# Two transformer-like blocks on one core: second projections in pieces between the seven products of a block of the first projection

## The chip, the core and the metric

One core of a Trainium2 chip runs the whole program in one launch. The metric is the device time in microseconds (us) of that launch; lower is better. A core has TensorE (matmuls into PSUM), VectorE, ScalarE and GpSimd, and SyncE, which issues transfers; each engine executes its own queue in order, and the engines meet at semaphores.

## The reference, cut to what matters

Two models follow each other on 512 tokens of width 1024, each with two layers. A layer is a mixer (projections, recurrences, attention) and a feed-forward network. The networks are what the change is about:

```python
# first model, twice, D_FF = 3072
h = rms_norm(x, norm_ffn[l])
ff_g, ff_u = jnp.split(h @ ffn_up[l], 2, axis=-1)
ff_g = causal_dwconv(ff_g, ffn_conv_w[l], ffn_conv_b[l])     # 3 taps along the tokens
x = x + (jax.nn.gelu(ff_g) * ff_u) @ ffn_down[l]
# second model, twice, D_FF_2 = 2816
gu = h @ w_gate_up
x = x + (jax.nn.silu(gu[..., :D_FF_2]) * gu[..., D_FF_2:]) @ w_down
```

All is float32.

## The kernel before, in words

Every large product is made of three float32r matmuls: an operand v is split into a high half (ScalarE rounds it, line 361, tiles named wh, ffh, ...) and a low half (VectorE subtracts, line 369, wl, ffl, ...), and `three` (line 436) adds low x high, high x low and high x high into one PSUM bank.

**Order of work.** The program is written out by a planner at build time. `Issue` (line 98) keeps one clock for each engine and a price for every instruction; of the instructions whose inputs are ready it appends, time after time, the one that could start first, and among those within 0.03 us of that the one of the lowest priority number. So prices and priorities fix the order of every engine's queue. A matmul's price stands in `mmr` (line 431), the priorities in `PRIO` (line 70).

**Units.** The weights come as a list of units, which `drive` (line 556) takes in order with four chains: a loader (SyncE loads a chunk of weights into one of 8 raw buffers, at most 8 units ahead), a splitter (line 593; wh and wl, three buffers each, freed when the unit's matmuls are done), the matmuls (`main`, line 603) and an evacuator (line 625), which hands on a unit's results when slots are free. A split has priority 1 when at least two of the three buffers are free (`split`), and 4 otherwise (`split2`). What follows a product goes into a chain called `behind`, of priority 0.

**A network** (`ffn`, line 1884). The first projection yields column blocks of 256 gate and 256 up columns, 12 blocks in the first model's networks, 11 in the second's. Blocks 0 and 1 are plain. The others (`Block`, line 1792) use a scheme of seven products, P1 to P7, of half size: 24 matmuls of 256 columns each into a bank ps_u. The weights of four of them are made in place: when the buffer has been split, GpSimd issues a transfer that adds another block of the matrix to it (`dma_add`), and the next product that uses the buffer splits it again. P1, P5, P6 and P4 use one buffer in this order, with an add after each of the first three; P7's buffer gets one add before its split.

A block's P1, P2, P5 and P6 alternate with P7, P4 and P3 of the block before, in the loop from line 1942:

```python
            yield B.u["P1"]
            if prev:
                yield prev.u["P7"]
            for d in todo:
                yield from down_units(*d, fs, False)
            todo = []
            yield B.u["P2"]
```

then P5, P4 and P3 of the block before, and P6. After P4, `after_P4` (line 1862) adds into the gate (fg) and calls the gate's `rest`: in the first model ScalarE's first tap, two VectorE taps (fy) and a gelu, in the second a silu. After P3, `after_P3` (line 1870) subtracts into u, multiplies u by the gate and splits the result into ffh and ffl, 128 rows of the second projection's input: two such tiles for a block.

**The second projection** (`down_units`, line 1914) runs on groups of tiles, (6, 6, 6, 6) in the first model and (6, 6, 6, 4) in the second. For a group it makes units of `proj_t` (line 644), each with two banks ps_t of 128x512; for 6 tiles a bank takes two units of 18 matmuls, for 4 tiles one unit of 24. VectorE adds a finished bank to x (x<-x,ps_t). All units of a group follow each other, behind P7.

Of the kernel before, what the change touches and what calls it, by code (L numbers as in the profile page):

```python
# [319 lines left out]
class Unit:  # L320


    def __init__(self, chunk, view, mm, evac=None, ready=None, pre=None, need=4):
        self.chunk, self.view, self.mm, self.evac, self.ready, self.pre = chunk, view, mm, evac, ready, pre
        self.need, self.w, self.then = need, None, None
        chunk.users += 1
# [3 lines left out]
def kernel(ctx, tc, a, out):  # L330
# [100 lines left out]
    def mmr(o, lhsT, rhs, first, last, **kw):  # L431
        order.op("pe", size(rhs) * 0.000445 + 0.004,
                 lambda: nc.tensor.matmul(o, lhsT=lhsT, rhs=rhs, start=first, stop=last, **kw), [o], [lhsT, rhs],  # L433
                 rows=lhsT.shape[0])
# [113 lines left out]
    behind = Chain(None, 0)  # L548

    def after(fn):  # L550

        old, order.cur = order.cur, behind
        fn()
        order.cur = old

    def drive(units):
# [36 lines left out]
        def splitter():  # L593
            for u in each():
                if u is None:
                    yield "wait"
                else:
                    yield from until(lambda: u.chunk.buf is not None and whs.left and wls.left)
                    order.cur.prio = PRIO["split2" if len(whs.left) < NHL - 1 else "split"]
                    split(u)  # L600
                    yield

        def main():
            q = 0
            while st["main"] < len(look) or not st["done"]:
                fill()
                u = look[st["main"]]
                q += 1
                if q in starts:
                    yield from starts[q]  # L610
                if u.pre is not None:
                    yield from u.pre()
                yield from until(lambda: u.w is not None)
                yield from u.mm(u.w[2], u.w[3])
                u.w[0].free()
                u.w[1].free()
                if u.evac is not None:
                    evacs.append(u)
                look[st["main"]] = None
                st["main"] += 1  # L620
                fill()
                yield
            st["over"] = True

        def evacuator():
            while True:
                while not evacs:
                    if "over" in st:
                        return
                    yield "wait"  # L630
                u = evacs.popleft()
                yield from until(lambda: (u.ready is None or u.ready()) and len(slots.left) >= u.need)
                after(u.evac)
                yield
# [9 lines left out]
    def proj_t(w, c0, ntile, src, evac, ready=None, pre=None, ktiles=8, need=3):  # L644

        for i0 in range(0, ntile, 2):
            n = min(2, ntile - i0)
            pss = {}
            if ktiles <= 4:
# [10 lines left out]
                def ev4(i0=i0, n=n, pss=pss):  # L660
                    for i in range(n):
                        evac(i0 + i, pss[i].t)
                        pss[i].free()

                yield Unit(ch, lambda ch=ch: ch.view(), mm4, ev4, ready, pre, need * n)
# [3 lines left out]
            for k0 in range(0, ktiles, kc):  # L669
# [12 lines left out]
                def ev8(i0=i0, n=n, pss=pss):  # L682
                    for i in range(n):
                        evac(i0 + i, pss[i].t)
                        pss[i].free()

                yield Unit(ch, lambda ch=ch: ch.view(), mm8, ev8 if k0 + kt == ktiles else None, ready, pre, need * n)
                pre = None

    def proj_n(w, c0, ncols, src, evac, ready=None, pre=None, ktiles=8, nb=NT):  # L690
# [3 lines left out]
        for k0 in range(0, ktiles, hs):  # L694
# [19 lines left out]
            yield Unit(ch, lambda ch=ch: ch.view(), mm_, ev if k0 + kt == ktiles else None, ready, pre, 0)  # L714
# [366 lines left out]
    def first_mix(l, norm, nxt):  # L1081
# [126 lines left out]
        def unit_small():  # L1208
# [14 lines left out]
            yield Unit(ch, lambda: ch.view(), mm_, lambda: spawn(small_chain(bank[0], r), PRIO["sm"]), rdy if r else None,  # L1223
# [568 lines left out]
    class Block:  # L1792
# [3 lines left out]
        def __init__(self, X, w, cols, gate, done):  # L1796
# [7 lines left out]
            for nm, ch, x, add in (("P1", A, "A11", b12), ("P5", A, "S1", b22), ("P6", A, "S2", b21), ("P4", A, "A22", None),  # L1804
                                   ("P7", T3, "S3", None), ("P2", C21, "A12", None), ("P3", C22, "S4", None)):
                u = self.u[nm] = Unit(ch, ch.view, lambda h, lo, nm=nm, x=x: self.mm(nm, x, h, lo))
                if add is not None:
                    u.then = lambda ch=ch, add=add: dma_add(ch.view(), add)
# [53 lines left out]
        def after_P4(self):  # L1862
# [3 lines left out]
            self.s1.free()  # L1866
            for j in range(2):
                self.g[j] = self.gate.rest(j, self.g[j])

        def after_P3(self):  # L1870
# [3 lines left out]
            self.u2.free()  # L1874
            for j in range(2):
# [8 lines left out]
    def ffn(norm, up, down, ff, groups, gate, fin, late=None):  # L1884
# [55 lines left out]
        prev, todo = None, []  # L1940
        spawn(X.build(norm), 3)
        for b in range(nblk):
            if b < NOLD:
                yield from plain(b, fs)
                continue
# [10 lines left out]
            for d in todo:  # L1956
                yield from down_units(*d, fs, False)
            todo = []
            yield B.u["P2"]
            yield B.u["P5"]  # L1960
# [3 lines left out]
            yield B.u["P6"]  # L1964
            prev = B
            if b - 1 in ends:
                todo.append(ends[b - 1])
        for nm in ("P7", "P4", "P3"):
            yield prev.u[nm]
        for d in todo:  # L1970
            yield from down_units(*d, fs, False)
# [688 lines left out]
    def body():  # L2660
        norm = norm0
        for l in range(2):
# [3 lines left out]
            yield from ffn(nf, a["ffn_up"][l], a["ffn_down"][l], FF1, (6, 6, 6, 6), lambda k0, l=l: Gate1(l, k0), norm.add,  # L2666
                           mem_prep if l == 1 else None)
        for l in range(2):
# [3 lines left out]
            yield from ffn(nf, a["w_gate_up_2"][l], a["w_down_2"][l], FF2, (6, 6, 6, 4), lambda k0: Gate2(),  # L2672
# [32 lines left out]
```

## Time and profile before

| | |
|---|---|
| median of 3 runs | 3403.86 us (3395.11 to 3408.48) |
| the profiled execution, its own time | 3401.47 us |
| its span, first to last instruction | 3399.7 us |
| mean granted TensorE clock | 0.983 |
| busy: TensorE (PE) | 3263.6 us, 96% |
| busy: VectorE (DVE) | 2175.3 us, 64% |
| busy: ScalarE (ACT) | 1574.1 us, 46% |
| busy: GpSimd (POOL) | 358.7 us, 11% |
| moved by DMA | 380.52 MB |

PE is the matmuls and PEld the weight loads of TensorE. A stretch with a granted clock of 1.00 ran at 2.4 GHz throughout, one of 0.50 at 1.2 GHz. Matmuls overlap in the profile, so the duration of one comes from the length of a run of them divided by their number, not from the mean of one. The networks lie at about 640 to 1000, 1640 to 2000, 2400 to 2730 and 3050 to 3400 us; the mixers lie between.

### The profile page before, as it was taken

To read this page: it belongs to the slowest core of one execution; us is meant where nothing else is said; L and a number is where in the kernel's file an instruction comes from. 1 tells how busy PE (TensorE), PEld (TensorE's weight loads), DVE (VectorE), ACT (ScalarE), POOL (GpSimd) and SP (SyncE) were. 2 spreads that over 40 slices of the span, in tenths; PEclk is the share of its full clock that TensorE was granted. 3 is DMA by queue.
4 is the path that set the end of the run, shared out by engine and by line. 5 is a ranking of instruction groups with operands and counts; after the bars stand their busy time and mean duration, and the time that the engine had idled before them with its cause. 6 is when DMAs were issued, how large, how long until landed. Compare 5 with 4: busy or idle time off the path is not lost. (4 is left out here: it accounts for less than half of the span.)

```text
span 3399.7 us, 45909 instructions
## 1 busy us (share of the span) xinstructions
PE 3263.6 (96%) x17637; PEld 2747.4 (81%) x17637; DVE 2175.3 (64%) x4134; ACT 1574.1 (46%) x2711; POOL 358.7 (11%) x407
## 2 busy tenths in 40 slices
PE   9999999999999999999899999999999999999999
PEld 6778778888887778778788888767888878888887
DVE  7973544765677973535765587776655577874554
ACT  6452433443344552433443366766433357743342
POOL 2000000111100000000111112110111111101110
PEclk9999999999999999999999999999999999999999
DMA  4323133466752323132476653211567642236773
GB/s 147 99 69 93 50 106 98 101 154 146 158 131 75 108 63 95 48 112 93 104 158 155 148 135 121 93 51 55 131 148 160 172 142 69 63 86 144 153 158 87
DMA packets 350667, 380.52 MB, mean 112 GB/s; under 512 B 17839, under 2 KB 324768, under 8 KB 350448
## 3 DMA queue, kind: packets, MB, share of 16 engines
q1 hardware_dynamic: 262576, 276.47, 26.3%
q0 software_dynamic: 87840, 101.12, 17.3%
q8 instruction: 138, 2.26, 0.3%
q14 instruction: 81, 0.66, 0.1%
q10 hardware_dynamic: 32, 0.01, 0.0%
HBM read 367.05 MB, written 10.49 MB: 111 GB/s over the span
## 5 line engine op out<-in xcount | busy, mean ns | idle before, releaser
L369 DVE TENSOR_TENSOR wl<-raw,wh 128x1024 fp32r<-128x1024 f32 (+2 forms) x667 | 775.5, 1167 | 675.5 <-ACT wh L361 673.9
L361 ACT ACTIVATE wh<-raw 128x1024 fp32r<-128x1024 f32 (+2 forms) x667 | 672.7, 1014 | 953.3 <-PE ps_t L433 496.9
L433 PE MATMUL ps_u<-xsh,wl 128*128 128x256 f32 x1216 | 363.0, 299 | 91.3 <-DVE wl L369 84.7
L433 PE MATMUL ps_u<-xsh,wh 128*128 128x256 f32 x1216 | 357.4, 294 | 0.0
L433 PE MATMUL ps_u<-xsl,wh 128*128 128x256 f32 x1216 | 357.2, 294 | 0.0
L433 PEld LDWEIGHTS ps_u<-xsh,wl 128*128 128x128 f32 x1216 | 245.0, 201 | 100.9 <-DVE wl L369 91.0
L433 PE MATMUL ps_t<-ffl,wh 128*128 128x512 f32 x736 | 290.4, 395 | 1.5 <-DVE ffl L369 1.5
L433 PE MATMUL ps_t<-ffh,wl 128*128 128x512 f32 x736 | 289.9, 395 | 0.6 <-ACT ffh L361 0.5
L433 PE MATMUL ps_t<-ffh,wh 128*128 128x512 f32 x736 | 290.3, 395 | 0.0
L433 PE MATMUL ps_t<-h2l,wh 128*128 128x512 f32 x704 | 283.8, 403 | 0.0
L433 PE MATMUL ps_t<-h2h,wl 128*128 128x512 f32 x704 | 283.7, 403 | 0.0
L433 PE MATMUL ps_t<-h2h,wh 128*128 128x512 f32 x704 | 281.3, 400 | 0.0
L433 PEld LDWEIGHTS ps_u<-xsl,wh 128*128 128x128 f32 x1216 | 245.8, 202 | 0.0
L433 PEld LDWEIGHTS ps_u<-xsh,wh 128*128 128x128 f32 x1216 | 245.8, 202 | 0.0
L369 DVE TENSOR_TENSOR x<-x,ps_t 128x512 f32<-128x512 f32 x192 | 131.0, 685 | 107.1 <-PE ps_t L433 106.9
L433 PE MATMUL ps_u<-xbh,wl 128*128 128x256 f32 x608 | 172.1, 283 | 6.8 <-DVE wl L369 3.8
L433 PE MATMUL ps_u<-xbl,wh 128*128 128x256 f32 x608 | 171.3, 282 | 0.0
L433 PE MATMUL ps_u<-xbh,wh 128*128 128x256 f32 x608 | 170.8, 281 | 0.0
L416 POOL DMA_DIRECT2D raw<-in_ffn_up_dram x80 | 102.3, 1363 | 630.0 <-DVE wl L369 486.5
L433 PEld LDWEIGHTS ps_t<-ffl,wh 128*128 128x128 f32 x736 | 138.2, 188 | 34.7 <-DVE ffl L369 3.0
L433 PEld LDWEIGHTS ps_t<-ffh,wl 128*128 128x128 f32 x736 | 138.1, 188 | 33.0 <-ACT ffh L361 1.1
L433 PEld LDWEIGHTS ps_t<-ffh,wh 128*128 128x128 f32 x736 | 138.2, 188 | 31.6
(453 smaller groups left out, 7271.0 us busy)
## 6 DMA issues: line engine op xcount, KB each, us to landing
raw<-in_w_in_dram SPq DMA_DIRECT2D x128, 512.0 KB, 3.8
raw<-in_ffn_up_dram SPq DMA_DIRECT2D x96, 512.0 KB, 3.5
raw<-in_w_gate_up_dram SPq DMA_DIRECT2D x88, 512.0 KB, 3.6
raw<-in_ffn_up_dram POOLq DMA_DIRECT2D x80, 512.0 KB, 6.0
raw<-in_w_gate_up_dram POOLq DMA_DIRECT2D x72, 512.0 KB, 6.5
raw<-in_ffn_down_dram SPq DMA_DIRECT2D x64, 384.0 KB, 5.1
raw<-in_w_out_dram SPq DMA_DIRECT2D x40, 512.0 KB, 3.4
raw<-in_w_down_dram SPq DMA_DIRECT2D x48, 384.0 KB, 5.3
```

Of the source, the lines that this page charges most:

```text
L361: lambda: nc.scalar.activation(out=out, in_=in_, func=func, **kw),
L369: dve(0.00104, lambda: nc.vector.tensor_tensor(out=out, in0=in0, in1=in1, op=op), [out], [in0, in1])
L416: order.op("pool", 1.0, lambda: nc.gpsimd.dma_start(out=out, in_=in_, accum_op=ALU.add), [out], [out], extra=max(n, 0.05), slack=0.5)
L433: lambda: nc.tensor.matmul(o, lhsT=lhsT, rhs=rhs, start=first, stop=last, **kw), [o], [lhsT, rhs],
```

## The change

- The loop over the blocks yields one unit of the second projection after P2 and one after P6, as long as the list `todo` has any (`between`). A group goes on that list right after P6 of the block that follows its last block; groups of the plain blocks at once.
- The groups are of four tiles: six in the first model, (4, 4, 4, 4, 6) in the second.
- The split of a product's weights always has priority 1 (`soon`).
- `rest` of the gate (convolution, gelu or silu) and the multiplies and splits after P3 move from `behind` into a chain `later` of priority 2.
- A unit's evacuation is a list with one entry for a tile; each waits for its own slots.
- The planner's price of a matmul of n columns is max(256, n)/2400 + 0.0025 us instead of 0.000445 n + 0.004: 0.2158 instead of 0.2318 for 512 columns, 0.1092 instead of 0.1179 for 256.

```diff
-        order.op("pe", size(rhs) * 0.000445 + 0.004,
+        order.op("pe", max(256, size(rhs)) / 2400.0 + 0.0025,
...
-    behind = Chain(None, 0)
-
-    def after(fn):
-
-        old, order.cur = order.cur, behind
+    behind, later = Chain(None, 0), Chain(None, 2)
+
+    def after(fn, chain=behind):
+
+        old, order.cur = order.cur, chain
...
-                    order.cur.prio = PRIO["split2" if len(whs.left) < NHL - 1 else "split"]
+                    order.cur.prio = PRIO["split2" if len(whs.left) < NHL - 1 and not u.soon else "split"]
...
-                if u.evac is not None:
-                    evacs.append(u)
+                for f in u.evac or ():
+                    evacs.append((u, f))
...
                 u = self.u[nm] = Unit(ch, ch.view, lambda h, lo, nm=nm, x=x: self.mm(nm, x, h, lo))
+                u.soon = True
...
             self.b3.free()
             self.s1.free()
+            after(self.gates, later)
+
+        def gates(self):
             for j in range(2):
                 self.g[j] = self.gate.rest(j, self.g[j])
...
             self.b4.free()
             self.u2.free()
+            after(self.ends, later)
+
+        def ends(self):
...
+        def between():
+
+            while todo:
+                u = next(todo[0], None)
+                if u is not None:
+                    return [u]
+                todo.popleft()
+            return []
+
...
-            for d in todo:
-                yield from down_units(*d, fs, False)
-            todo = []
             yield B.u["P2"]
+            yield from between()
             yield B.u["P5"]
...
             yield B.u["P6"]
+            if b - 1 in ends and b - 1 >= NOLD:
+                todo.append(down_units(*ends[b - 1], fs, False))
+            yield from between()
             prev = B
-            if b - 1 in ends:
-                todo.append(ends[b - 1])
...
-            yield from ffn(nf, a["ffn_up"][l], a["ffn_down"][l], FF1, (6, 6, 6, 6), lambda k0, l=l: Gate1(l, k0), norm.add,
+            yield from ffn(nf, a["ffn_up"][l], a["ffn_down"][l], FF1, (4,) * 6, lambda k0, l=l: Gate1(l, k0), norm.add,
...
-            yield from ffn(nf, a["w_gate_up_2"][l], a["w_down_2"][l], FF2, (6, 6, 6, 4), lambda k0: Gate2(),
+            yield from ffn(nf, a["w_gate_up_2"][l], a["w_down_2"][l], FF2, (4, 4, 4, 4, 6), lambda k0: Gate2(),
```

SyncE's queue in the first network: the loads of first (ffn_up) and second (ffn_down) projection. Before:

```order
L410 DMA raw<-in_ffn_up_dram 128x4x256 x16
L410 DMA raw<-in_ffn_down_dram 128x3x256 x8
L410 DMA raw<-in_ffn_up_dram 128x4x256 x12
L410 DMA raw<-in_ffn_down_dram 128x3x256 x8
L410 DMA raw<-in_ffn_up_dram 128x4x256 x8
```

Now, its beginning:

```order
L410 DMA raw<-in_ffn_up_dram 128x4x256 x10
L410 DMA raw<-in_ffn_down_dram 128x4x256 x2
L410 DMA raw<-in_ffn_up_dram 128x4x256 x3
L410 DMA raw<-in_ffn_down_dram 128x4x256
L410 DMA raw<-in_ffn_up_dram 128x4x256
L410 DMA raw<-in_ffn_down_dram 128x4x256
L410 DMA raw<-in_ffn_up_dram 128x4x256 x4
```

Eight down loads in a row have become single ones between one to four up loads.

VectorE's queue in the last network, around the split for P6 of block 6. Before, where that split is wl_28476, the bank of P4 ps_u_28477, and the bank of P5 and P3 ps_u_28199:

```order
L369 TENSOR_TENSOR fg_28161<-ps_u_28477,s1_28099 128x256
L369 TENSOR_TENSOR fg_28162<-ps_u_28477,s1_28099 128x256
L369 TENSOR_TENSOR u_28374<-ps_u_28199,u2_28293 128x256
L369 TENSOR_TENSOR u_28375<-ps_u_28199,u2_28293 128x256
L369 TENSOR_TENSOR u_28374<-u_28374,fg_28161 128x512
L369 TENSOR_TENSOR u_28375<-u_28375,fg_28162 128x512
L369 TENSOR_TENSOR wl_28476<-raw_28062,wh_28475 128x1024
L369 TENSOR_TENSOR ffl_28505<-u_28374,ffh_28504 128x512
```

Now, where P6's split is wl_28498, the next down unit's wl_28536, the next P1's wl_28564, and the banks are ps_u_28499 (P4) and ps_u_28158 (P5 and P3):

```order
L369 TENSOR_TENSOR wl_28498<-raw_28055,wh_28497 128x1024
L369 TENSOR_TENSOR fg_28086<-ps_u_28499,s1_28021 128x256
L369 TENSOR_TENSOR fg_28087<-ps_u_28499,s1_28021 128x256
L369 TENSOR_TENSOR wl_28536<-raw_28331,wh_28535 128x1024
L369 TENSOR_TENSOR u_28362<-ps_u_28158,u2_28257 128x256
L369 TENSOR_TENSOR u_28363<-ps_u_28158,u2_28257 128x256
L369 TENSOR_TENSOR u_28362<-u_28362,fg_28086 128x512
L369 TENSOR_TENSOR wl_28564<-raw_28364,wh_28563 128x1024
L369 TENSOR_TENSOR ffl_28527<-u_28362,ffh_28526 128x512
```

The split for P6 has moved from behind the subtractions after P3 and the multiplies to ahead of the additions after P4; a multiply and its ffl now stand between later splits.

The first down unit of a fresh group, in the first network after P6 of block 6 (bank ps_t_6697 and ps_t_6698, weights wh_6634 and wl_6635; tiles ff_6309 and ff_6311 are old, ff_6623 and ff_6625 come from the block whose P3 stands just before P6). VectorE's queue now, from the end of that P3 on (fy are the taps, wl_6662 the split for P1, wl_6704 for P7):

```order
L369 TENSOR_TENSOR u_6457<-ps_u_6245,u2_6347 128x256
L373 SCALAR_TENSOR_TENSOR fy_6595<-fg_6173,colt2_97,fy_6595 128x510
L369 TENSOR_TENSOR u_6458<-ps_u_6245,u2_6347 128x256
L369 TENSOR_TENSOR wl_6662<-raw_6459,wh_6661 128x1024
L369 TENSOR_TENSOR u2_6664<-ps_u_6663,s1_6422 128x512
L373 SCALAR_TENSOR_TENSOR fy_6596<-fg_6174,colt3_98,fy_6596 128x511
L369 TENSOR_TENSOR wl_6704<-raw_6492,wh_6703 128x1024
L373 SCALAR_TENSOR_TENSOR fy_6596<-fg_6174,colt2_97,fy_6596 128x510
L369 TENSOR_TENSOR u_6457<-u_6457,fy_6595 128x512
L369 TENSOR_TENSOR u_6458<-u_6458,fy_6596 128x512
L369 TENSOR_TENSOR ffl_6624<-u_6457,ffh_6623 128x512
L369 TENSOR_TENSOR ffl_6626<-u_6458,ffh_6625 128x512
```

Before, three products (P6, P1, P7) stood between the end of such a P3 and the first matmul of a group. TensorE's queue in that unit now, from the last of twelve matmuls on old tiles:

```order
L433 MATMUL ps_t_6698<-ffh_6311,wh_6634 128x512
L433 MATMUL ps_t_6697<-ffh_6623,wl_6635 128x512
L433 MATMUL ps_t_6698<-ffh_6623,wl_6635 128x512
L433 MATMUL ps_t_6697<-ffl_6624,wh_6634 128x512
L433 MATMUL ps_t_6697<-ffh_6623,wh_6634 128x512
L433 MATMUL ps_t_6697<-ffh_6625,wl_6635 128x512
```

The twelve matmuls on old tiles of both banks stand first, and the matmuls on the fresh tiles follow. There are four such units in each of the first model's networks and three in each of the second's, where eighteen matmuls stand ahead of those on the last tile (in the first of the three, eighteen in another order).

## Rows read from the trace of the kernel before

**Rows 1.** Busy time by stage: mixer and network in turn; columns below.

```profile
core 0: us, PE busy (x) PEld busy (x) DVE busy (x) ACT busy (x) POOL busy (x), PEclk, DMA share, GB/s
0.00:640.00 640.00, 625.10 (x2845) 491.94 (x2846) 407.96 (x881) 285.68 (x486) 40.78 (x85) 0.99 0.31 95
640.00:1000.00 360.00, 332.06 (x2186) 306.28 (x2184) 220.73 (x301) 148.64 (x196) 49.79 (x39) 0.96 0.65 145
1000.00:1640.00 640.00, 635.39 (x2863) 496.48 (x2862) 397.55 (x811) 273.43 (x455) 24.05 (x49) 0.99 0.29 86
1640.00:2000.00 360.00, 331.72 (x2203) 305.38 (x2202) 225.83 (x311) 151.55 (x199) 56.01 (x49) 0.97 0.67 148
2000.00:2400.00 400.00, 391.19 (x1908) 313.49 (x1907) 315.98 (x846) 271.21 (x640) 57.13 (x67) 1.00 0.26 81
2400.00:2730.00 330.00, 308.20 (x2024) 282.42 (x2023) 183.81 (x252) 121.67 (x168) 51.63 (x46) 0.97 0.68 155
2730.00:3050.00 320.00, 317.30 (x1524) 257.64 (x1523) 243.11 (x502) 200.73 (x407) 35.10 (x38) 1.00 0.28 89
3050.00:3400.00 350.00, 322.65 (x2097) 293.80 (x2095) 180.37 (x236) 121.24 (x163) 44.18 (x35) 0.97 0.61 135
```

**Rows 2.** Waits of TensorE, whole span: us in total, times, longest.

```profile
PE ps_u L433 <- DVE wl L369: 88.5, 33, 4.8
```

**Rows 3.** Chain of waits, 2540 to 2670: start, length, what.

```profile
2554.48 33.44 PE ps_t L433 x144
2587.92 31.27 PE ps_u L433 x264
...
2619.22 0.48 DVE u L369 x2
...
2620.49 0.68 DVE u L369
2621.17 1.15 DVE wl L369
...
2622.36 16.10 PE ps_u L433 x120
```

**Rows 4.** Busy time over a stretch with two waits; columns as in rows 1.

```profile
2619.00:2659.00 40.00, 33.57 (x243) 32.93 (x242) 23.34 (x31) 15.40 (x21) 7.67 (x6) 0.87 0.70 139
```

**Rows 5.** Timeline of VectorE and GpSimd, a split and the add after it.

```profile
2606.59 1.23 DVE L369 TENSOR_TENSOR wl<-raw,wh 128x1024 fp32r<-128x1024 f32 x1 [1.25 <-ACT wh L361]
...
2608.11 1.26 POOL L416 DMA_DIRECT2D raw<-in_w_gate_up_dram  x1 [6.45 <-DVE wl L369]
```

**Rows 6.** DMA issues, 2588 to 2659, products only: KB, median us to landing.

```profile
raw<-in_w_gate_up_dram POOLq DMA_DIRECT2D x10, 512.0 KB, 6.3
...
raw<-in_w_gate_up_dram SPq DMA_DIRECT2D x5, 512.0 KB, 5.6
```

**Rows 7.** DMA issues, 2554 to 2659, a down projection and products.

```profile
raw<-in_w_gate_up_dram SPq DMA_DIRECT2D x12, 512.0 KB, 3.6
```

**Rows 8.** Groups by form, 755 to 870: busy us, mean ns of one, idle before.

```profile
L369 DVE TENSOR_TENSOR wl<-raw,wh 128x1024 fp32r<-128x1024 f32 x23 | 27.9, 1220 | 11.5 <-ACT wh L361 11.5
L361 ACT ACTIVATE wh<-raw 128x1024 fp32r<-128x1024 f32 x24 | 25.3, 1054 | 17.6 <-PE ps_t L433 9.6 <-PE ps_u L433 3.4 <-issue 3.4
...
L373 DVE SCALAR_TENSOR_TENSOR fy<-fg,colt,fy 128x511 f32<-128x511 f32 x8 | 5.8, 750 | 1.7 <-ACT fy L361 1.7
...
L369 DVE TENSOR_TENSOR x<-x,ps_t 128x512 f32<-128x512 f32 x8 | 5.5, 686 | 6.2 <-PE ps_t L433 6.2
...
L369 DVE TENSOR_TENSOR u<-u,fy 128x512 f32<-128x512 f32 x6 | 3.9, 682 | 0.0
L361 ACT ACTIVATE ffh<-u 128x512 fp32r<-128x512 f32 x6 | 3.7, 628 | 2.1 <-DVE u L369 2.1
L369 DVE TENSOR_TENSOR u<-ps_u,u 128x256 f32<-128x256 f32 x8 | 3.2, 417 | 0.0
```

**Rows 9.** Instructions that write wl, whole span: ns min/median/max, forms.

```profile
L369 DVE TENSOR_TENSOR wl<-raw,wh x667: 557/1218/1258, 9.4 to 3375.6; 128x1024 fp32r<-128x1024 f32 x134, 128x768 fp32r<-128x768 f32 x29, 128x640 fp32r<-128x640 f32 x2, 128x384 fp32r<-128x384 f32 x2
```

More of the change, by code (lines that the diff above doesn't have):

```diff
@@ L324, in __init__ @@
         self.chunk, self.view, self.mm, self.evac, self.ready, self.pre = chunk, view, mm, evac, ready, pre
-        self.need, self.w, self.then = need, None, None
+        self.need, self.w, self.then, self.soon = need, None, None, False
         chunk.users += 1
@@ L630, in evacuator @@
                     yield "wait"
-                u = evacs.popleft()
+                u, f = evacs.popleft()
                 yield from until(lambda: (u.ready is None or u.ready()) and len(slots.left) >= u.need)
-                after(u.evac)
+                after(f)
                 yield
@@ L658, in mm4, with ev4 @@
                                   s[k].h, s[k].l, k == 0, k == ktiles - 1)
[L660 to L665, printed above, removed]
+                def ev4(i, i0=i0, pss=pss):
+                    evac(i0 + i, pss[i].t)
+                    pss[i].free()
+                yield Unit(ch, lambda ch=ch: ch.view(), mm4, [lambda i=i, ev=ev4: ev(i) for i in range(n)], ready, pre, need)
                 pre = None
@@ L680, in mm8, with ev8 @@
                                   s[k0 + k].h, s[k0 + k].l, k0 + k == 0, k0 + k == ktiles - 1)
[L682 to L687, printed above, removed]
+                def ev8(i, i0=i0, pss=pss):
+                    evac(i0 + i, pss[i].t)
+                    pss[i].free()
+                yield Unit(ch, lambda ch=ch: ch.view(), mm8,
+                           [lambda i=i, ev=ev8: ev(i) for i in range(n)] if k0 + kt == ktiles else None, ready, pre, need)
                 pre = None
@@ L712, in ev @@
                     evac(tb, pss[tb])
-            yield Unit(ch, lambda ch=ch: ch.view(), mm_, ev if k0 + kt == ktiles else None, ready, pre, 0)
+            yield Unit(ch, lambda ch=ch: ch.view(), mm_, [ev] if k0 + kt == ktiles else None, ready, pre, 0)
             pre = None
@@ L1222, in unit_small @@
             r = raw[0]
-            yield Unit(ch, lambda: ch.view(), mm_, lambda: spawn(small_chain(bank[0], r), PRIO["sm"]), rdy if r else None,
+            yield Unit(ch, lambda: ch.view(), mm_, [lambda: spawn(small_chain(bank[0], r), PRIO["sm"])], rdy if r else None,
                        swapped())
@@ L1939, in ffn @@
         nblk = k0 // 2
-        prev, todo = None, []
+        prev, todo = None, deque()
         spawn(X.build(norm), 3)
+        def between():
[5 more added lines that the diff above has]
+            return []
         for b in range(nblk):
@@ L1944, in ffn @@
                 yield from plain(b, fs)
+                if b in ends:
+                    todo.append(down_units(*ends[b], fs, False))
                 continue
@@ L1964, in ffn @@
             yield B.u["P6"]
+            if b - 1 in ends and b - 1 >= NOLD:
+                todo.append(down_units(*ends[b - 1], fs, False))
+            yield from between()
             prev = B
-            if b - 1 in ends:
-                todo.append(ends[b - 1])
         for nm in ("P7", "P4", "P3"):
             yield prev.u[nm]
-        for d in todo:
-            yield from down_units(*d, fs, False)
+        while todo:
+            yield from between()
         yield from down_units(*ends[nblk - 1], fs, True)
```

## The prediction

> **What bounds the kernel now.** I read the busy times by stage first. TensorE is busy 625.10 of 640 us in the first mixer, and nearly as fully in the other three (635.39 of 640, 391.19 of 400, 317.30 of 320): about 31 us of idle in 2000. The four feed-forward stages are different: 332.06 of 360, 331.72 of 360, 308.20 of 330 and 322.65 of 350, some 105 us idle in 1400, and they alone have a mean granted clock of 0.96 or 0.97 [rows 1]. So TensorE bounds the kernel everywhere, and what can be won without removing matmuls lies in the feed-forward stages.
>
> Next, the waits of TensorE. One kind stands out: ps_u (a product, which only those stages have) waiting for wl, the low half of a weight split: 88.5 us in 33 waits [rows 2]. The chain of waits shows how one is made [rows 3]. After a down projection of 144 matmuls, 264 product matmuls run through without a gap (31.27 us). Then TensorE stops at 2619.2 and goes on at 2622.36: VectorE does two u subtractions, the multiplies by the gate, and only then wl, the split that the next product (P6) needs. The wait is VectorE's order: the split stands behind work that waits for TensorE itself. The clock pays again: over 2619 to 2659, with two such waits, the granted clock is 0.87, so part of that stretch ran at 1.2 instead of 2.4 GHz [rows 4].
>
> There is a second limit near by. A product's weights are made by adding into a buffer in place, so P6's split waits for an add that P5's split releases: that split ran at 2606.59 for 1.23 us, GpSimd issued the add at 2608.11 [rows 5], and adds land a median 6.3 us after issue [rows 6]. 2608.1 + 6.3 = 2614.4, under 5 us before TensorE wanted P6. During 71 us with products only, the loads of SyncE take 5.6 us to land [rows 6].
>
> **The change, part by part.**
>
> *Splits of product weights always at priority 1; gating and the ends at priority 2.* No instruction is added. The order of VectorE shows it: in the last network wl for P6 stood behind both subtractions and both multiplies; now it stands ahead of them and of the gate additions that wait for P4. The wait of [rows 3] goes wherever the split's data are there in time.
>
> *Two down units of 24 matmuls between the seven products of a block.* A down matmul takes 33.44 / 144 = 0.232 us, a unit 5.57 us; a product takes 31.27 / 264 x 24 = 2.84 us [rows 3]. A block goes from 19.9 us to 31.0. With three buffers for split weights, P5 may be split when P7 of the block before has ended, and P6 is wanted P2 + down unit + P5 + P4 + P3 later: 4 x 2.84 + 5.57 = 16.9 us. The split (1.05 + 1.22 us [rows 8]), 0.3 us to the issue and 6.3 us for the add end after 8.9 us, the second split at 11.2: about 5.7 us to spare. Without a unit between, P5's split could begin at P1's end, 14.2 us ahead, leaving 3 us, which VectorE's order then ate. So in the regular blocks both causes go.
>
> Two blocks of each network aren't regular: the first with products (P5 directly before P6) and block 4, where no group is ready between P2 and P5. There a wait between 0 and today's 3.2 us stays; I take 1 us each, as the data come about when they are wanted: 8 us in all, bounds 0 and 26. Removed: 88.5 - 8 = **80.5 us**.
>
> *A new wait.* A group of two blocks is put on the list right after P6 of the block that follows it, and a unit comes at once. Its last two tiles are only finished after P3, one product earlier. In the networks with convolution, VectorE has after P3's end (time 0), in the printed order: u, a tap, u, wl (0.42 + 0.75 + 0.42 + 1.22 = 2.81), the addition of 512 columns that waits for P6's end at 2.84 (as a multiply of that size, 0.68), a tap 0.75, wl 1.22, a tap 0.75, two multiplies of 0.68; at 6.92 the first u is there, ScalarE's ffh 0.63 later at 7.55, VectorE's ffl, as long as a multiply, at 8.28 [rows 8]. TensorE has P6 (2.84) and the twelve matmuls on old tiles (2.78), done at 5.62. It waits 7.55 - 5.62 = 1.93 and then about 0.3 for ffl: 2.2 us. In the other two networks eighteen matmuls are put first (7.0 us), and the last u, without convolution, gives ffh at 6.6: no wait. Four such units in each of the first two networks: 8 x 2.2 = **17 us** back. Bounds: 0, and 3.8 us at all 14 places (8 + 2 x 3), 53 us, if nothing covers it.
>
> Here a rule of the Trainium skill differs from the rows. The page "TensorE: Matmul & The Clock Gate", section "Back-to-back issue gap", gives 512 columns an isolated spacing of about 216 ns. The rows have 232. By the page a down unit would be 5.18 us and the fresh wait some 0.4 us longer, the sum 3 us higher; the rows decide.
>
> *The clock.* The rounded clocks say 0.04 x 720 + 0.03 x 680 = 49 us of full speed missing in these stages [rows 1]. Some of that lies inside the waits and is counted there, so I take 40. It should shrink as the waits do, 17 + 8 us for 88.5, and short waits cost less clock: about 8 us remains. **32 us** gained, bounds 15 and 40.
>
> *Groups of four.* 48 more x<-x,ps_t (192 before; two more groups of eight in networks 1 and 2, one more in 3 and 4), 0.686 us each: 33 us of VectorE [rows 8], which is busy 811 of 1400 us in these stages [rows 1]. Priced at nothing; they follow finished units, whose weights have been split, and without the cover they cost up to 33 us. Matmuls: the same number. Splits: 24 of 1024 columns for 32 of 768, about equal in engine time.
>
> *Evacuation tile by tile.* Frees a bank earlier; nothing waits for banks in the rows: 0.
>
> *The plan's price of a matmul.* Matmuls are priced some 7% lower, so every order in the mixers is drawn up anew. No row shows such an order. I take 0, with -15 and +30 as bounds: half and all of the 31 us idle there, and the middle because the waits that the mixers have now can move either way.
>
> *Loads.* A block now takes six chunks through the eight raw buffers instead of four. Each load still gets its buffer about a block (31 us) ahead, against 3.6 us to land [rows 7]: no price.
>
> **Sum**, against the profiled execution's 3401.47 us (2.4 us under the median of three runs, 3403.86, whose spread is 13): 3401.5 - 80.5 + 17 - 32 = **3306 us**. u and s waits at the start and the end of a network (about 9 us) stay.
>
> **Rivals.**
>
> 1. *The wait moves to the fresh down unit.* All 14 places cost 3.8 us and 1.5 us of clock (49 us over 33 waits today): 74 us instead of 17 + 8, or 49 us worse: 3355. For it: splits now overtake the work that finishes the tiles. Against: TensorE's own order puts old tiles first. Chance 0.10.
>
> 2. *The adds come later and nothing is won.* If the down loads stretch an add from 6.3 to twice that, P5's split plus add end 15.2 us after P7's end, P6's split at 17.5 instead of 16.9, and once late it meets VectorE's queue again: 2 to 3 us a block in 38 blocks, about what is lost today: 3392. For it: SyncE's loads land in 5.6 us among products [rows 6] and in 3.6 us over the longer stretch [rows 7]. Against: loads and adds per us fall, since a block is 31 us long instead of 20 plus a burst. The Trainium skill, page "DMA: Bandwidth & Descriptors", section "Issuing engines are not separate DMA queues", says that transfers started by different engines interleave on the same 16 DMA engines; by that the rival's loads would indeed slow the adds, and the trace's 5.6 against 3.6 agrees. Chance 0.07.
>
> 3. *Slower: the plan is drawn for a TensorE faster than the real one.* The new price makes a 5.57 us unit 0.39 us shorter in the plan. VectorE then holds instructions that wait for a matmul's end ahead of a split that could have run. 667 splits [rows 9] less 266 of products are 401 units; at 0.39 us each, 156 us, less the gain of 95: 3462. It decides when more than 0.6 of these come through the three buffers of split weights. Against: the mixers' units follow each other closely now with VectorE 62 to 79% busy [rows 1]. The section of the Trainium skill named above gives the very spacing that the new price uses; the trace's 232 ns disagrees with it. Chance 0.05.
>
> That the change doesn't reach the queues is excluded: SyncE's order has down loads between up loads.
>
> **Numbers.** The forecast has 0.78. Within 0.5%, some 17 us, a measurement of this kernel can't tell a difference. Faster by more: forecast and rival 1, 0.88; within: rival 2, 0.07; slower: rival 3, 0.05. The range reaches from 3278 (the bounds of clock and leftover waits on the good side) to 3362 (rival 1 with a little more).
>
> **What would show it.** Right: TensorE's waits on wl in the product stages fall from 33 to about 8 and under 15 us; ps_t waits on ffh or ffl appear, 8 of about 2 us in the first two networks; the clocks there reach 0.98 or more; idle in the mixers stays near 31 us. Wrong: wl waits of 3 us stay (rival 2, if wh waits for the DMA before them), ps_t waits near 50 us (rival 1), or mixers with more than 60 us idle (rival 3).

## The result, and the profile after

The changed kernel takes 3283.4 us (median of 4 runs, 3281.3 to 3285.01) against 3404.3 (4 runs, 3395.11 to 3408.48): a ratio of 0.9648, 95% interval 0.9628 to 0.9669. Forecast were 3306, range 3278 to 3362. The profiled execution takes 3284.13 us, span 3282.4, granted clock 0.993.

To see where the time went, both spans are cut at the first product (ps_u) and the last matmul of the second projection (ps_t<-ffh or ffl) of each network. Kernel before, busy time of the four networks and of the third mixer (its columns: length, PE, PEld, DVE, ACT, POOL, granted clock, DMA share, GB/s):

```profile
647.60:1024.10 376.50, 348.56 (x2256) 319.67 (x2255) 229.78 (x310) 157.67 (x209) 48.50 (x38) 0.96 0.65 145
...
1659.30:2034.20 374.90, 346.47 (x2272) 316.86 (x2271) 239.45 (x343) 165.20 (x228) 56.96 (x49) 0.97 0.65 147
2034.20:2407.40 373.20, 364.54 (x1786) 292.32 (x1785) 287.41 (x787) 248.81 (x598) 56.19 (x67) 1.00 0.26 82
2407.40:2743.20 335.80, 314.00 (x2056) 287.30 (x2056) 192.65 (x267) 129.67 (x184) 50.34 (x45) 0.97 0.66 154
...
3055.30:3393.50 338.20, 316.16 (x2069) 288.97 (x2068) 176.80 (x232) 118.94 (x160) 43.39 (x34) 0.97 0.61 135
```

The changed kernel, all eight stages (the answer to [rows 1]):

```profile
0.00:645.60 645.60, 633.30 (x2877) 498.09 (x2878) 414.15 (x891) 289.28 (x491) 44.14 (x86) 0.99 0.32 95
645.60:993.10 347.50, 338.09 (x2256) 308.34 (x2255) 241.77 (x323) 158.26 (x201) 48.31 (x38) 0.99 0.70 156
993.10:1622.90 629.80, 626.09 (x2842) 491.46 (x2841) 398.19 (x818) 270.18 (x450) 28.76 (x50) 0.99 0.29 86
1622.90:1968.20 345.30, 335.93 (x2256) 307.00 (x2256) 243.16 (x338) 160.27 (x210) 54.60 (x48) 1.00 0.70 158
1968.20:2350.30 382.10, 371.77 (x1803) 302.03 (x1802) 294.24 (x803) 254.01 (x608) 57.95 (x68) 0.97 0.26 80
2350.30:2658.50 308.20, 305.34 (x2056) 279.74 (x2056) 199.81 (x273) 131.01 (x182) 50.24 (x45) 1.00 0.73 167
2658.50:2967.60 309.10, 308.05 (x1482) 252.02 (x1481) 233.25 (x483) 194.19 (x390) 33.04 (x38) 1.00 0.30 91
2967.60:3276.40 308.80, 305.93 (x2068) 280.18 (x2068) 183.12 (x236) 119.34 (x157) 43.25 (x34) 1.00 0.67 149
```

The networks are 1309.8 us long instead of 1425.4. Of the 115.6, 75.7 are idle time of TensorE (lengths less PE busy: 100.2 before, 24.5 after), and 39.9 are busy time: the same matmuls ran at a higher granted clock (0.96 and 0.97 before, 0.99 and 1.00 after). The mixers together are nearly unchanged; the third is 8.9 us longer, at a clock of 0.97.

Waits of TensorE in the changed kernel (us in total, times, longest), beside [rows 2]:

```profile
PE ps_t L433 <- ACT ffh L361: 12.4, 8, 1.7
PE ps_u L433 <- DVE wl L369: 4.6, 4, 1.6
PE ps_n L433 <- DVE wl L369: 4.3, 1, 4.3
```

88.5 us on wl have become 4.6, and the new wait on fresh tiles (ffh) is there, eight times. The chain of waits in the last stretch of products of the third network, beside [rows 3] (start, length, what):

```profile
2556.72 8.53 PE ps_u L433 x72
2565.25 5.58 PE ps_t L433 x24
2570.83 11.40 PE ps_u L433 x96
2582.22 5.57 PE ps_t L433 x24
2587.80 8.53 PE ps_u L433 x72
2596.32 5.58 PE ps_t L433 x24
```

A whole block, 31.07 us from 2565.25 to 2596.32, has no gap: a down unit, four products, a down unit, three products.

### The profile page after: what moved, and what is told of

It is laid out like the page before. It is cut to its first block, busy times and chain, and to the rows that moved or that the text cites. A ratio compares the mean times of both kernels' runs of the same rounds, so it can differ in the third digit from the quotient of the medians.

```text
span 3282.4 us, 45761 instructions
## 1 busy us (share of the span) xinstructions
PE 3225.6 (98%) x17637; PEld 2719.3 (83%) x17637; DVE 2208.4 (67%) x4158; ACT 1577.3 (48%) x2685; POOL 360.3 (11%) x407
## 4 chain that ended last, share of the span: by engine, by line
PE 92%; DVE 5%; issue 2%; ACT 1%; DMA 0%; SPq 0%; POOL 0%; DVEq 0%; ACTq 0%; POOLq 0%
PE ps_t L433 45%; PE ps_u L433 23%; PE ps_n L433 12%; PE ps_at L433 2%; PE ps_y L433 2%; PE ps_pt L425 2%; PE ps_at L421 1%; PE ps_y L421 1%; DVE wl L369 1%; ACT pr L361 1%; DVE score L1239 1%; DVE m L1238 1%; PE ps_num L421 1%; PE ps_S L421 1%; DVE u L369 0%
## 5 line engine op out<-in xcount | busy, mean ns | idle before, releaser
L369 DVE TENSOR_TENSOR wl<-raw,wh 128x1024 fp32r<-128x1024 f32 (+1 forms) x643 | 776.6, 1209 | 566.4 <-ACT wh L361 564.3
L361 ACT ACTIVATE wh<-raw 128x1024 fp32r<-128x1024 f32 (+1 forms) x643 | 671.4, 1047 | 888.8 <-PE ps_t L433 387.0
L433 PE MATMUL ps_u<-xsh,wl 128*128 128x256 f32 x1216 | 342.1, 281 | 7.4 <-DVE wl L369 4.6
L433 PE MATMUL ps_u<-xsl,wh 128*128 128x256 f32 x1216 | 341.6, 281 | 0.0
L433 PE MATMUL ps_u<-xsh,wh 128*128 128x256 f32 x1216 | 341.2, 281 | 0.0
L433 PE MATMUL ps_t<-ffh,wl 128*128 128x512 f32 x736 | 289.2, 397 | 12.5 <-ACT ffh L361 12.4
L369 DVE TENSOR_TENSOR x<-x,ps_t 128x512 f32<-128x512 f32 x240 | 163.8, 686 | 157.7 <-PE ps_t L433 157.2
L433 PEld LDWEIGHTS ps_u<-xsh,wl 128*128 128x128 f32 x1216 | 229.2, 188 | 10.8 <-DVE wl L369 5.4
L433 PEld LDWEIGHTS ps_u<-xsl,wh 128*128 128x128 f32 x1216 | 228.9, 188 | 1.6
L433 PEld LDWEIGHTS ps_u<-xsh,wh 128*128 128x128 f32 x1216 | 229.3, 189 | 0.0
L433 PE MATMUL ps_n<-wl,hh 128*128 128x512 f32 (+2 forms) x416 | 163.9, 394 | 4.4 <-DVE wl L369 4.3
```

Of the source, the lines that this page charges most:

```text
L361: lambda: nc.scalar.activation(out=out, in_=in_, func=func, **kw),
L369: dve(0.00104, lambda: nc.vector.tensor_tensor(out=out, in0=in0, in1=in1, op=op), [out], [in0, in1])
```

## The experiments

**First, which part does it.** Three theories: the order of the queues and the cover, which is the down unit between the products, both count (A, that of the prediction); the cover is all that counts (B); the priorities are all (C). Four kernels were run against 3404.69 us (7 runs).

*The priorities alone, on the kernel before.*

```diff
+    behind, later = Chain(None, 0), Chain(None, 2)
...
+                    order.cur.prio = PRIO["split2" if len(whs.left) < NHL - 1 and not u.soon else "split"]
...
+                u.soon = True
...
+            after(self.gates, later)
...
+            after(self.ends, later)
```

> The kernel before, with the priorities of the change alone: splits of product weights always 1, gating and the work after P3 in the chain of priority 2. Theory A (order and cover both count: the split for P6 stands behind work on VectorE, and its data also come late): P5's split still begins at P1's end, so 3 us are to spare and the order no longer eats them; waits of ps_u on wl fall from 88.5 us to 25 to 40, time 3330 to 3350. Theory B (the down unit between is all that counts): no gain, 3395 to 3410. Theory C (the order is all that counts): as the change, 3280 to 3300.

Measured: 3370.77 us, ratio 0.9896 (0.9877 to 0.9914). Waits of TensorE:

```profile
PE ps_u L433 <- DVE wl L369: 76.1, 35, 3.8
```

Most of the waits stay, and the time is in none of the three ranges, though 34 us shorter. The waits are of two kinds, which stand next to each other in the third network (below: start, duration, engine, instruction, idle before it and what ended that). The first kind is at P6 of a block that follows another directly:

```profile
2596.98 0.75 ACT L361 ACTIVATE fg<-fg 128x256 f32<-128x256 f32 x2 [4.53 <-DVE fg L369]
2597.63 1.99 ACT L361 ACTIVATE wh<-raw 128x1024 fp32r<-128x1024 f32 x2
...
2599.35 0.76 DVE L369 TENSOR_TENSOR u<-ps_u,u 128x256 f32<-128x256 f32 x2 [2.07 <-PE ps_u L433]
2600.02 1.22 DVE L369 TENSOR_TENSOR wl<-raw,wh 128x1024 fp32r<-128x1024 f32 x1
...
2601.29 0.39 PE L433 MATMUL ps_u<-xsh,wl 128*128 128x256 f32 x1 [1.98 <-DVE wl L369]
```

The add that this split needs was issued at 2588.30 and landed 6.6 us later, 4.4 us before TensorE wanted P6. It is the order that costs here: ScalarE stood 4.53 us before the gate's silu, with the splits for P3 and P6 behind it, and VectorE's part of the split stands behind the subtractions after P3. The second kind comes four products later, at P5 of the next block:

```profile
2604.10 1.22 DVE L369 TENSOR_TENSOR wl<-raw,wh 128x1024 fp32r<-128x1024 f32 x1
...
2603.27 2.57 POOL L416 DMA_DIRECT2D raw<-in_w_gate_up_dram  x2 [0.46 <-DVE wl L369]
...
2613.16 1.06 ACT L361 ACTIVATE wh<-raw 128x1024 fp32r<-128x1024 f32 x1 [5.29 <-DMA raw<-in_w_gate_up_dram]
...
2614.25 1.23 DVE L369 TENSOR_TENSOR wl<-raw,wh 128x1024 fp32r<-128x1024 f32 x1 [2.65 <-ACT wh L361]
...
2615.53 0.38 PE L433 MATMUL ps_u<-xsh,wl 128*128 128x256 f32 x1 [2.62 <-DVE wl L369]
```

ScalarE stood 5.29 us for an add that P1's split had released and that landed 9.8 us after its issue, VectorE 2.65 for ScalarE, TensorE 2.62 for VectorE: here the data are late. Of the 33 waits over half a us, 13 are such chains from a transfer (28.7 us); in the other 20 (46.9 us) the split follows another instruction of VectorE without a pause. The kernel before has 8 (20.3 us) and 22 (66.7 us), and one of another kind. So the priorities alone don't bring the splits forward at P6. C falls, and A's count of 25 to 40 us with it; what a better order without cover would give was not run.

*The interleaving and the groups of four alone*, with the old priorities, price and evacuation.

```diff
-            for d in todo:
-                yield from down_units(*d, fs, False)
-            todo = []
             yield B.u["P2"]
+            yield from between()
...
+            if b - 1 in ends and b - 1 >= NOLD:
+                todo.append(down_units(*ends[b - 1], fs, False))
+            yield from between()
```

> The kernel before, with the down units between the products and groups of four alone: old priorities, old price of a matmul, evacuation of all tiles at once. Theory A: the data for P6's split come 5.7 us early, but at priority 4 it still gets behind the gate's work in part of the blocks: ps_u waits on wl 15 to 40 us, time 3310 to 3340; the fresh down units wait less than in the change, as the work after P3 keeps priority 0. Theory B: as the change, 3280 to 3295. Theory C: wl waits stay near 88 us and the time near 3400.

Measured: 3272.56 us, ratio 0.9611 (0.9593 to 0.963), faster than the whole change. TensorE's waits on wl:

```profile
PE ps_u L433 <- DVE wl L369: 5.6, 2, 2.8
```

No wait on ffh. ScalarE's splits of up-projection weights wait 27.3 us for a DMA in the whole program (11 times) instead of 57.0 (25 times) before. Both kinds of wait are nearly gone, with the old priorities. B holds, further than it asked: what comes on top costs some 11 us.

*The change with the old price of a matmul*, and *the change without both priorities*.

> The change with the old price of a matmul (0.2318 us for 512 columns). If the price counts for nothing: 3278 to 3290, with waits as in the change. If the new, too low price hurts the plan (the slower rival in small): 5 to 20 us faster, above all in the mixers. If the lower price helps, because VectorE's work is put earlier against TensorE's: 5 to 20 us slower, with more wl waits.

Measured: 3286.89 us, ratio 0.9652 (0.9634 to 0.9669): no difference to the change as a whole (3283.4 us).

> The change without its priorities: product splits at 1 or 4 as before, gating and the work after P3 at 0. Theory A: wl waits come back in part, 15 to 40 us instead of 4.6, fresh down units wait 0 to 6 us instead of 12.4; 3295 to 3325. Theory B: 3280 or a little less, as the fresh units no longer wait. Theory C: near 3400.

Measured: 3286.17 us, ratio 0.9647 (0.9626 to 0.9668): none to the change either, but the waits are others: 22.6 us on wl in 10, under 1 us on the fresh tiles. The priorities trade one kind for the other.

**Second, where the down units must stand.** Four kernels against 3403.5 us (10 runs). Theory D: the add is late, so only a unit between P2 and P5 helps. Theory S: anything spread between the products helps.

*The interleaving alone, both units between P2 and P5; both behind P6.*

> The kernel before with the down units interleaved and groups of four, as in e3_between, but both units of a block stand between P2 and P5 and none behind P6. Theory D (the add is what is late: a down unit helps only where it stands between the point that frees P5's split and P6): the add for P6 gets another 5.6 us, no wait of TensorE on wl is left in the regular blocks, under 6 us of them in all; a fresh group is first taken a whole P1 and P7 after its tiles, so no wait on ffh or ffl. 3265 to 3276 us. Theory S (any work that is spread between the products gives VectorE its time, wherever it stands): the same as e3_between, 3273, for another reason; this kernel alone doesn't tell them apart, the next one does.

Measured: 3295.73 us, ratio 0.9689 (0.9672 to 0.9706).

> As e9_p2twice, but both down units of a block stand behind P6 and none between P2 and P5. Theory D: between the point that frees P5's split and P6 there are products alone again, 14.2 us, so the waits on wl come back, 60 to 90 us in 30 to 38 places, with the clock's share: 3350 to 3400 us. Theory S: the same TensorE work is spread over the block, so the waits stay away, 3270 to 3300 us.

Measured: 3320.1 us, ratio 0.9758 (0.9737 to 0.9779). Waits in the second of these:

```profile
PE ps_u L433 <- DVE wl L369: 22.0, 11, 4.8
PE ps_t L433 <- DVE wl L369: 9.8, 18, 1.0
```

Both theories miss in time. With both units behind P6 no wait on wl in a regular block is over 1 us; the long ones stand at the first block with products (4.7 and 4.8 us in networks 1 and 2) and at the end of a network. With both at P2 there is one wait of 3.2 to 3.8 us a network, some 72 us after its start. So D is wrong: 14.2 us of products ahead of P6 are enough once a down unit has stood anywhere in the block. S is right for the waits of regular blocks. The even spread was best; why these two kernels are 23 and 48 us slower than it was followed no further than these waits. An estimate from [rows 5], [rows 6] and [rows 8] shows why the place matters little: splits go in the units' order, so from one P6's split to the next stand the split for P1, an add, the split for P5, an add and the split for P6, 1.22 + 6.6 + 2.27 + 6.6 + 2.27 = 19 us. That is nearly all of a block of 19.9 us, and leaves 12 us in one of 31.0, wherever its down units stand.

*Groups of four alone*, a group's units still together.

```diff
-            FF1, (6, 6, 6, 6)
+            FF1, (4,) * 6
...
-            FF2, (6, 6, 6, 4)
+            FF2, (4, 4, 4, 4, 6)
```

> The kernel before with groups of four tiles alone: the down units of a group still stand together between P7 and P2. Theories D and S: a group of four every second block in place of six every third changes nothing of what stands between P2 and P6, so the waits on wl stay, 70 to 95 us: 3390 to 3420 us, with the 33 us of additional VectorE adds hidden or partly not. Rival (the shorter groups themselves give the gain, by freeing tiles sooner): under 3340 us.

Measured: 3387.21 us, ratio 0.9955 (0.994 to 0.997). Waits:

```profile
PE ps_u L433 <- DVE wl L369: 71.5, 22, 5.0
```

Somewhat less than foreseen, and the reason teaches: stretches of two blocks have one such wait, where stretches of three have two [rows 4] (here in the third network at 2487.4, 2554.5 and 2622.6, a group of down units between each two). The block that follows a down group is free of it; the block that follows a block directly has it. At its end stands VectorE's order, as in [rows 3]: in 18 of the 22 the split follows other work without a pause. But with the units interleaved the same priorities give it at two places only, the 5.6 us of the first such kernel. So this order comes where there is no cover; that the planner's prices make it is argued, not shown.

*The interleaving with the evacuation tile by tile.*

> e3_between with the evacuation tile by tile added, nothing else (old priorities, old price). e3_between was 3272.6 and e5_noprio, which has this and the new price, 3286.2 us. Theory E (the evacuation tile by tile costs the 11 to 13 us, by the later start of the third mixer above all): 3280 to 3288, third mixer about 380 us long and with a wait of 4 us or more at its start. Rival (the new price costs them): 3270 to 3276, third mixer about 372 us.

Measured: 3268.25 us (3266.21 to 3272.92), ratio 0.9612 (0.9595 to 0.963), the same as without it within the spread. The evacuation costs nothing, though the third mixer was 378 us long. So the loss of the change against this kernel comes from price and priorities, and they don't add: the price alone costs 18 us on top of it (3286.17), the priorities alone 19 (3286.89), both together 15.

VectorE's timeline at the same place of the first network shows an order that changes with the price. With the old price:

```profile
843.43 0.76 DVE L369 TENSOR_TENSOR fg<-ps_u,s 128x256 f32<-128x256 f32 x2 [0.52 <-PE ps_u L433]
844.52 1.22 DVE L369 TENSOR_TENSOR wl<-raw,wh 128x1024 fp32r<-128x1024 f32 x1 [0.34 <-ACT wh L361]
845.67 2.73 DVE L373 SCALAR_TENSOR_TENSOR fy<-fg,colt,fy 128x511 f32<-128x511 f32 x4
848.31 0.42 DVE L369 TENSOR_TENSOR u<-ps_u,u 128x256 f32<-128x256 f32 x1
```

With the new price and no priorities (the kernel of e5_noprio):

```profile
843.41 0.76 DVE L369 TENSOR_TENSOR fg<-ps_u,s 128x256 f32<-128x256 f32 x2 [3.36 <-PE ps_u L433]
844.72 2.78 DVE L373 SCALAR_TENSOR_TENSOR fy<-fg,colt,fy 128x511 f32<-128x511 f32 x4 [0.56 <-ACT fy L361]
847.42 0.42 DVE L369 TENSOR_TENSOR u<-ps_u,u 128x256 f32<-128x256 f32 x1
847.75 1.22 DVE L369 TENSOR_TENSOR wl<-raw,wh 128x1024 fp32r<-128x1024 f32 x1
...
849.03 0.39 PE L433 MATMUL ps_u<-xsh,wl 128*128 128x256 f32 x1 [2.81 <-DVE wl L369]
```

The split for P6 has fallen behind four taps and an instruction that waits for P3's end: the wait of [rows 3] again, 2.81 us.

**Third, the rest of the loss.** Three kernels against 3401.39 us (7 runs), and one against 3402.51 (7 runs).

*The change, with a group put on the list one unit later.*

```diff
+            yield from between()
             if b - 1 in ends and b - 1 >= NOLD:
                 todo.append(down_units(*ends[b - 1], fs, False))
-            yield from between()
```

> The changed kernel, with one line moved: a group of down units comes on the list after the unit that follows P6 has been taken, so its first unit stands between P2 and P5 of the next block, a P1, a P7 and a P2 (8.5 us) after the tiles were begun to be finished. Theory F (the eight waits on ffh in networks 1 and 2, 12.4 us, are the fresh tiles and nothing else): they go, and nothing takes their place: 3266 to 3273 us. Rival (the wait is that VectorE is short of time, and comes back on wl or in the last units of a network, where one more unit is left over): the same sum of waits, 3279 to 3288 us.

Measured: 3257.9 us (3257.5 to 3258.72), ratio 0.9578 (0.9562 to 0.9594). That is below both ranges. The waits on ffh are gone; on wl TensorE waits 7.9 us in 6. One line is worth 25 us, twice the 12.4 of the waits, but it is not all theirs: the first network is 10.0 us shorter and the second 4.0 longer, the third mixer is 13.3 shorter, and the third and fourth networks, which had no such wait, are 3.5 and 2.7 shorter. The planner draws every later order anew.

*The interleaving and the evacuation, with late gates and ends but no early splits.*

> e11_evac (interleaving, groups of four, evacuation tile by tile; 3268 us) with one priority of the change added: gates and ends at 2, while the splits keep their old rule. Theory L (it is the late gating that makes the fresh tiles late): waits on ffh or ffl of 8 to 13 us in eight places of networks 1 and 2 appear, 3278 to 3288 us. Rival (it is the splits at priority 1 that push the tiles back): no such waits, 3266 to 3272 us.

Measured: 3300.79 us, ratio 0.9704 (0.9689 to 0.9718). Neither theory: no waits on ffh, but these:

```profile
PE ps_t L433 <- DVE wl L369: 25.6, 7, 6.1
```

Now the split of a down unit's own weights is late, about 3.25 us at six places and 6.06 at one, all in networks 1 and 2. What orders that split so late was not followed further.

*The change with early splits only.*

> The changed kernel without the priority of gates and ends (2 back to 0); the splits keep priority 1 and the new price stays. e5_noprio, without both, had 22.6 us of waits on wl and none on ffh; the changed kernel, with both, has 4.6 and 12.4. Theory L (the late gates and ends make the fresh tiles late, the splits at 1 mend the waits on wl): waits on wl under 8 us and no waits on ffh: 3258 to 3270 us. Rival (splits that overtake push the tiles back by themselves): waits on ffh stay at 10 to 13 us: 3279 to 3288 us. A third way (the splits at 1 alone reach nothing, because the gates stand ahead of them all the same): waits on wl stay at 15 to 23 us, 3280 to 3290 us.

Measured: 3290.1 us, ratio 0.9671 (0.9655 to 0.9687): the third way. Waits on wl stay at 20.4 us in 7, none on ffh. Alone neither priority helped (the early splits under the new price, the late gates under the old); under the new price both together mend wl and make the fresh tiles late.

*The interleaving and the evacuation, with the new price in the mixers only.*

```diff
-        order.op("pe", size(rhs) * 0.000445 + 0.004,
+        order.op("pe", size(rhs) * 0.000445 + 0.004 if dear[0] else max(256, size(rhs)) / 2400.0 + 0.0025,
...
+                dear[0] = u.dear
                 yield from u.mm(u.w[2], u.w[3])
+                dear[0] = False
```

> e11_evac with the new price of a matmul in the mixers alone, the old one in the feed-forward stages. From the stages of e5_noprio and e11_evac: the new price shortened the mixers by 2.1, 6.7 and 2.8 us and lengthened the third by 3.8, and lengthened the networks by 5.9 to 8.4 us each. Theory M (each price does its work in its own stages): networks as in e11_evac (338, 338, 305, 307), mixers as in e5_noprio (645, 628, 382, 309): 3258 to 3264 us. Rival (the mixers' differences are only another draw of the order, or hang on where the network before has ended): 3265 to 3275 us.

Measured: 3258.45 us (3256.38 to 3258.97), ratio 0.9578 (0.9564 to 0.9592), as Theory M foresaw. The networks stay within 2 us of those without the new price, and mixers 1, 2 and 4 are 4.8, 8.1 and 2.9 us shorter, the third 1.3 longer. With the kernel above this is the fastest; both beat the change by 25 us.

## Why the prediction was right

The sign, the place and the range held; the change is 22 us faster than forecast. That the range held is in part luck: the bounds that it names at its lower end, of the clock and of the leftover waits, give 3306 - 8 - 8 = 3290 us, above the measured 3283.4, and no sum there leads to 3278. And the interleaving with groups of four alone takes 3272.56 us: the other parts, counted as a gain or as nothing, cost 11 us together. Against the profiled execution's 3401.5 us the sum had -95.5, and the change took 117.3: idle in the networks -75.7 instead of -63.5, busy time there -39.9 instead of -32, mixers -1.5 instead of 0.

- **Removed waits** (80.5 us, 8 left): 83.9, 4.6 left in 4 places. The size is right, and that a block with down units has no such wait is shown. Of "So in the regular blocks both causes go" the half on the priorities is not: the interleaving without them leaves 5.6 us, the priorities without it 76.1. The slack of 3 us without a unit, "which VectorE's order then ate", fits the waits at P6, where the data are in time and the order is not, and ScalarE's order has a part in it; it was worked out for P6 alone, and P5's data can be late too, 2.6 us at 2615.53 in the kernel with the priorities only. And 14.2 us of products ahead of P6 did suffice with both units behind P6.
- **The fresh tiles** (17 us, 8 times 2.2, none in networks 3 and 4): 12.4 us, 8 times 1.05 to 1.73, none in networks 3 and 4. The place was exact. VectorE, ScalarE and TensorE at one of them, from P6's end at 786.0:

```profile
786.20 0.69 DVE L369 TENSOR_TENSOR u<-ps_u,s 128x512 f32<-128x512 f32 x1 [0.24 <-PE ps_u L433]
786.80 0.74 DVE L373 SCALAR_TENSOR_TENSOR fy<-fg,colt,fy 128x511 f32<-128x511 f32 x1
787.46 1.22 DVE L369 TENSOR_TENSOR wl<-raw,wh 128x1024 fp32r<-128x1024 f32 x1
788.60 0.75 DVE L373 SCALAR_TENSOR_TENSOR fy<-fg,colt,fy 128x510 f32<-128x510 f32 x1
789.26 0.69 DVE L369 TENSOR_TENSOR u<-u,fy 128x512 f32<-128x512 f32 x1
...
789.98 0.63 ACT L361 ACTIVATE ffh<-u 128x512 fp32r<-128x512 f32 x1
...
790.66 0.49 PE L433 MATMUL ps_t<-ffh,wl 128*128 128x512 f32 x1 [1.72 <-ACT ffh L361]
...
791.45 0.19 PEld L433 LDWEIGHTS ps_t<-ffl,wh 128*128 128x128 f32 x1 [0.49 <-DVE ffl L369]
```

  Forecast was ffh 4.71 us after P6's end (7.55 - 2.84); it came at 790.61, 4.6 after. The 0.3 us for ffl is there too, as a wait of the weight load: the third matmul starts 0.79 us after the first, where two take 0.46. Rival 1, 3.8 us at all 14 places, did not come. Its mechanism, splits that overtake the work on the tiles, is seen at 787.46, but early splits alone made no such wait, only early splits with late gates. That moving one line gave 25 us, as much as the 17 plus 8 that the forecast had kept for these waits and the clock, is a coincidence: the first two networks, where the waits are, gained 6.0 us of it together.
- **The clock** (32 us of 40): 39.9 of busy time, 8 more. The 8 kept back were too many; the granted clock is 0.99 in the first network and 1.00 in the others. The 49 us behind the 40 were misread: [rows 1] has 0.96 for the first network only, and 0.04 x 360 + 0.03 x 1040 is 46.
- **48 more adds into x** (0, up to 33 us): VectorE's busy time in the networks rose from 838.7 to 867.9 us, and groups of four alone were no slower (3387.21 us, without cover): hidden, as costed.
- **Evacuation** (0): 3268.25 against 3272.56 us, 0.
- **The price** (0, -15 to +30): in the whole change 0, by the run that undoes it, but as a sum of two things. In the mixers alone it brings about 10 us, and without the priorities it lengthens the networks by 28 (1316.5 us in e5_noprio, 1288.4 in e11_evac), with them by about 5. Rival 3's mechanism exists without the priorities, at some ten splits of products and not at the 240 or so, of other units, that it needed.
- **Loads** (0) and rival 2: over the program, a median load of up-projection weights now lands after 4.7 or 4.5 us instead of 3.5 or 3.6, an add after 6.0 or 6.1 instead of 6.0 or 6.5. The adds did not come later, so rival 2 did not come. The Trainium skill, page "DMA: Bandwidth & Descriptors", section "Issuing engines are not separate DMA queues", lets transfers of different engines share the same 16 DMA engines; the loads agree with that, the adds show nothing of it.
- **Mixers** (idle stays near 31): 27.4 us. The third one starts with the wait on ps_n, 4.3 us; what follows ran at a low clock, 0.60 over 17 us:

```profile
1973.00:1990.00 17.00, 16.27 (x73) 15.99 (x74) 11.28 (x25) 7.66 (x15) 3.45 (x3) 0.60 0.37 105
```

  The third mixer was 366.6 to 384.2 us long over the kernels of this study; which edit sets that is left open.

## What to carry to other kernels

A wait whose last link is an engine's order need not be mended at that link. Here the order was written by a planner, and with other work between the products it wrote a good one by itself. Try such cover before priorities, and each alone: cover with the shorter groups gave 132 us, of which the groups alone give 16; the priorities alone gave 34, and on top of the cover they cost 19 at the old price and gave 3 at the new. Look at more than one wait before a kind is called the cause: two kinds stood 14 us apart here. When a unit may read something fresh, put one more unit ahead of it. A planner's price can be better in one stage and worse in another, so measure it by stage.

## What had not been expected of the hardware

Equal short waits cost unequal clock. After the 1.72 us wait at 790.66 the stretch around it has a granted clock of 0.89:

```profile
785.00:800.00 15.00, 13.22 (x72) 11.01 (x72) 9.29 (x12) 5.59 (x8) 2.54 (x2) 0.89 0.68 144
```

Three of the eight waits on fresh tiles have half-speed work right behind them, at 790.66, 856.61 and 1768.03; behind the wait of 1.73 us at 922.47 the clock stayed at 1.00. With all eight gone (the change with a group put on the list one unit later) the first network ran at 1.00 throughout:

```profile
645.60:983.10 337.50, 332.83 (x2256) 306.71 (x2255) 240.42 (x323) 157.58 (x201) 48.32 (x38) 1.00 0.71 160
```

Units of 24 matmuls of 512 columns take 5.57 or 5.58 us here too, 0.232 us each. The Trainium skill, page "TensorE: Matmul & The Clock Gate", section "Back-to-back issue gap", gives about 216 ns for an isolated matmul, which is near the new price of 0.2158, and about 131 ns for one in a stream of weight loads and matmuls. The trace shows neither, and yet the mixers gained by the new price.
